# Seven-product up-projection of a hybrid decoder layer: weight tiles counted one by one, parts of x and gated pieces formed and loaded at other places

## Chip, core and metric

The kernel runs on one core of a Trainium2 chip. The metric is the device time of one execution in microseconds (us); lower is better. TensorE (PE in the profile) does the matrix products, VectorE (DVE) and ScalarE (ACT) the elementwise work, GpSimd (POOL) a little, and SyncE (SP) issues most DMAs. Each engine executes its own instructions in the order in which the program lists them, and waits for the others through semaphores.

## The reference, cut to what matters

One decoder layer runs on 1024 prompt tokens and 8 single-token samples (T = 1024, TT = 1032 columns in all). The change touches the layer's second half: the layer norm after the mixers, a gated feed-forward network with a causal convolution of width 3, and the entry of its down-projection.

```python
x = layer_norm(ALPHA * x + mix, ln1_g, ln1_b)
hup = x @ w_up                                  # D_MODEL 1024 -> 2 * D_FF, D_FF = 2816 = 22 * 128
c = ext[:, 0:L]*conv_w[0] + ext[:, 1:L+1]*conv_w[1] + ext[:, 2:L+2]*conv_w[2] + conv_b
a, b = jnp.split(c, 2, axis=-1)
f = (jax.nn.gelu(a) * b) @ w_down
x = layer_norm(ALPHA * x + f, ln2_g, ln2_b)
```

## The kernel before, in words

**Products.** Activations stand transposed, features on partitions and the 1032 tokens in columns. Every fp32 operand is split into a high and a low part (`hi` by a copy on ACT, `lo = x - hi` on DVE), and each product is three matmuls: hi with hi, hi with lo, lo with hi. The tile `xhi`/`xlo` holds eight feature tiles of 1032 columns.

**Order of work.** The program is written by hand. A list of units (`run_units`) and later the loops `run_pairs` and `run_down` issue the matmuls. Two side lanes hold Python generators. `side.advance(us)` is called after about each 0.6 us worth of matmuls and gives both lanes that much credit; a generator's `yield 4.0` means "go on 4 us of TensorE work later". Evacuations of PSUM and the steps of the convolution (`post`) are issued at the end of each chunk of columns. So a yield sets only the place of an instruction in its engine's queue. When it runs is set by the queue ahead of it and by its operands.

**The layer norm** (`to_features`, L380 to L396). Rows are transposed by TensorE, scaled by ACT into `tmp` (L389), stored to DRAM (`x1D`, a DMA issued by ACT, L392), copied to `xhi` by ACT (L393) and subtracted to `xlo` by DVE (L394), for eight feature tiles in each of three passes over token columns. The up-projection of the columns starts when the last pass is through.

**Plain up-projection.** The first three of 22 column tiles (each with an a and a b half) are computed plainly, as units of 24 matmuls in each of three chunks (384, 384 and 264 columns). Here they are called 0a, 0b, 1a, 1b, 2a, 2b. Their PSUM tiles have the tag "d" with 3 buffers, so a chunk needs the evacuation (`hup`, ACT, L1524) of the third chunk before it. Before unit 1a, `open_ffn` opens the pools of this stage and puts `g_parts` in lane 0 and `g_first` in lane 1. Pool "wf" has NWF = 12 tiles.

**Seven-product up-projection.** The other 19 column tiles use a Strassen-like scheme: x and w are cut into 2 by 2 blocks and seven products (numbers 1 to 7) replace eight. `g_parts` forms the parts of x for products 6, 7 and 4 (tiles `tx`): for each of four feature tiles k it loads four quarters from `x1D` and forms differences on DVE (L1672 to L1680) and splits them (L1664 ACT, L1665 DVE). `last_part` (L1688 to L1693) splits the difference that product 5 needs into the right half of `xhi`/`xlo`, which unit 2b still reads. For a pair of column tiles (a and b) four weight tiles are loaded, three more are sums (DVE adds at L1585, L1588, L1590 and one in place at L1593), and `prepare()` splits one of the seven per call (L1600 ACT, L1601 DVE) into one of seven slots. A pair runs in two halves of 258 columns, each with products in the order 1, 2, (3 of the half before), 6, (4 of the half before), 7, 5. Products 6, 5 and 3 add onto the PSUM bank of product 1, and product 4 onto that of product 7, after what stood there has been read. The block in the lower right (`c22`, DVE, L1759) is read from the bank of product 7 before product 4 goes onto it.

**Counting.** `made["live"]` counts "wf" tiles. A pair counts 6 (four loads and two sums) from its load to its last prepare; nothing of it is loaded until all 6 fit.

**Down-projection.** The gated rows (`gD` in DRAM) are loaded in groups of four (`stage`, L1850) and split into `xhi`/`xlo` (L1854 ACT, L1855 DVE). For the first group the eight pieces are loaded into "wf" tiles and placed during the last half of the last pair (`early_stage`; L1870, L1874, L1875); the tiles of `x1D` for the residual (`z2`, L1862) are loaded there too, four at a time. `run_down` adds each output chunk onto `z2` (L1934, L1936).

Of the kernel before, what the change touches and what calls it, by code (L numbers as in the profile page):

```python
# [8 lines left out]
F32 = mybir.dt.float32  # L9
# [103 lines left out]
def tile_hybrid_step(ctx: ExitStack, tc: tile.TileContext, x_prompt, mem_prompt, x_sample, cache_mem_k,  # L113
# [1436 lines left out]
    wq, made = [], {"load": 0, "key": 0, "obj": 0, "step": 0, "live": 0}  # L1550
# [3 lines left out]
    class Weights:  # L1554


        def __init__(self, src, steps=(0,)):
            self.src, self.w, self.f, self.steps = src, {}, {}, steps
            self.nf = 6 if len(src) > 1 else 1
# [4 lines left out]
    def load_weights():  # L1564
        while made["load"] < len(wq) and made["live"] + wq[made["load"]].nf <= NWF:
            o = wq[made["load"]]
            for key, src in o.src.items():
                o.f[key] = wf_tile(src.shape[1] * 128)
                nc.sync.dma_start(o.f[key].rearrange("p (k c) -> p k c", c=128), src)
            made["live"] += o.nf  # L1570
            made["load"] += 1

    def prepare():
# [5 lines left out]
        if made["obj"] == made["load"]:  # L1579
            return False  # L1580
        if len(o.src) > 1:
            f, add = o.f, nc.vector.tensor_add
            if key == 1:
                f[5] = wf_tile()
                add(f[5], f[21], f[4])  # L1585
            elif key == 2:
                f[6] = wf_tile()
                add(f[6], f[5], f[1])  # L1588
            elif key == 6:
                add(f[21], f[1], f[21])  # L1590
                f[7] = f.pop(21)
            elif key == 3:
                add(f[2], f[2], f[6])  # L1593
                f[3] = f[2]
# [7 lines left out]
        o.w[key] = [x.rearrange("p (k c) -> p k c", c=128) for x in (hi, lo)] + [slot]  # L1602
        made["step"] += 1
        if made["step"] == len(o.steps):
            made["live"] -= o.nf
            o.f.clear()
            made["step"] = 0
            made["obj"] += 1
# [19 lines left out]
    def open_ffn():  # L1628
# [10 lines left out]
        made["live"] = 8  # L1639
# [8 lines left out]
    def g_parts():  # L1648
# [5 lines left out]

        def load(k):
            quarters[k] = []
            for a in range(2):
                for b in range(2):
                    x = wf_tile(HT)
                    nc.sync.dma_start(x, x1D[k + 4 * a][:, b * HT:(b + 1) * HT])  # L1660
                    quarters[k].append(x)
# [5 lines left out]
        load(0)  # L1667
        yield 4.0
        load_weights()
        for k in range(4):  # L1670
# [4 lines left out]
            yield 1.5  # L1675
            split(7, k, x22)
            V.scalar_tensor_tensor(x11, x22, -1.0, x11, op0=OP.mult, op1=OP.subtract)
            yield 1.7
            split(6, k, x11)
            V.scalar_tensor_tensor(x21, x11, -1.0, x21, op0=OP.mult, op1=OP.subtract)  # L1680
            yield 1.7
            split(4, k, x21)
            if k < 3:
                load(k + 1)
                yield 4.0
        made["live"] -= 4

    def last_part():  # L1688
        for k in range(4):
            h, l = xhi[:, k, HT:], xlo[:, k, HT:]  # L1690
            nc.scalar.activation(h, N1[k], AF.Copy)
            nc.vector.tensor_sub(l, N1[k], raw_f(h))
        made["live"] -= 4  # L1693
# [110 lines left out]
    def run_pairs():  # L1804
        before = None
        halves_ = [Half(u, s) for u in pairs for s in range(2)]
        for i, h in enumerate(halves_ + [None]):
            if i == len(halves_) - 3:
                made["live"] += 8
            for x, (m, old) in enumerate(ORDER):  # L1810
                hh = before if old else h
                if hh is None:
                    continue
# [3 lines left out]
                if m == 4 and hh.s:  # L1817
                    post.append(conv_pair(hh.u.j, hh.u.out))
                if x in (2, 3, 5, 6):
                    post[:] = [g for g in post if next(g, g) is not g]  # L1820
# [3 lines left out]
                if i == len(halves_) - 1:  # L1824
                    early_stage(m)
# [18 lines left out]
    def stage_load(gi, parts):  # L1844
        j0, nk = GROUPS[gi]
        if gi not in stage:
            stage[gi] = place["t"].tile([128, 4, TT], F32, tag="t", name=nm("stage"))
        for c0, c1 in parts:
            for k in range(nk):
                nc.sync.dma_start(stage[gi][:, k, c0:c1], gD[j0 + k][:, c0:c1])  # L1850

# [5 lines left out]
    def load_z2(fs):  # L1857
        for f in fs:
            if f % 4 == 0:
                Z2["t", f // 4] = place["t"].tile([128, 4, TT], F32, tag="t", name=nm("z2"))  # L1860
            Z2[f] = Z2["t", f // 4][:, f % 4]
            nc.sync.dma_start(Z2[f], x1D[f])  # L1862

    piece = {}

    def early_stage(m):

        def fetch(k, b):
            x = piece[k, b] = wf_tile(HT)
            nc.sync.dma_start(x, gD[k][:, b * HT:(b + 1) * HT])  # L1870

        def place_piece(k, b):
            c = slice(b * HT, (b + 1) * HT)
            nc.scalar.activation(xhi[:, k, c], piece[k, b], AF.Copy)  # L1874
            nc.vector.tensor_sub(xlo[:, k, c], piece[k, b], raw_f(xhi[:, k, c]))  # L1875

        if m == 1:
            assert made["live"] - 4 <= NWF, made
            for k in range(4):
                fetch(k, 0)  # L1880
        elif m == 2:
            assert made["live"] <= NWF, made
            for k in range(4):
                fetch(k, 1)
        elif m == 6:
            place_piece(0, 0)
            load_z2(range(4))
        elif m == 4:
            place_piece(1, 0)
        elif m == 7:  # L1890
            place_piece(2, 0)
            load_z2(range(4, 8))
        elif m == 5:
            place_piece(3, 0)
            for k in range(4):
                place_piece(k, 1)
            made["live"] -= 8
# [54 lines left out]
    downs[0].before = lambda: side.add(0, "stages", g_stages())  # L1952
# [69 lines left out]
    last_part()  # L2022
# [40 lines left out]
```

## Time and profile before

| what | value |
|---|---|
| median of 3 runs | 2209.15 us (2208.63 to 2210.41) |
| profiled execution | 2208.31 us, span of its instructions 2206.6 us |
| TensorE busy | 2135.5 us, 97% of the span |
| mean granted clock of TensorE | 0.984 of full speed |
| DVE, ACT busy | 1286.8 us (58%), 857.4 us (39%) |

TensorE is busy in all but 71 us of the span. The granted clock is the share of its full speed (2.4 GHz) that TensorE was given, and has two levels, full and half; a mean between them says how much of a stretch was at half.

### The profile page before, as it was taken

Reading aid. Unit: us, or ns where it says so; the run is one execution under the profiler, and the core shown is the slowest. Engines: PE = TensorE matmul, PEld = TensorE weight load, DVE = VectorE, ACT = ScalarE, POOL = GpSimd, SP = SyncE. Lnnn points to the kernel's source line nnn. Section 1 sums busy time; section 2 is a strip of 40 time slices with the busy share of each in tenths; the row PEclk is TensorE's granted clock in tenths of the full one; section 3 lists DMA queues with packets and bytes.
Section 4 is the critical chain, followed back from the end, with each engine's and each line's share of the span. In section 5 each row is a group of like instructions: output and inputs, shape, how many; then the busy total and the mean of one; then the engine's idle time right before and its main releaser. Section 6 shows DMA issues by size and latency. Waiting matters only on the chain.

```text
span 2206.6 us, 37536 instructions
## 1 busy us (share of the span) xinstructions
PE 2135.5 (97%) x14801; PEld 2088.6 (95%) x14801; DVE 1286.8 (58%) x2898; ACT 857.4 (39%) x1717; POOL 207.9 (9%) x329
## 2 busy tenths in 40 slices
PE   7999999999999999999999999998999999999996
PEld 7999999999998999899999999887999999899995
DVE  5734738373756754534335555556777777755357
ACT  4624343434446433332213334543445445522111
POOL 5301010101000000000005610000000000000004
PEclk8999999999999999999999999988999999999998
DMA  8231232223378665649644233333232232651302
GB/s 240 79 107 53 58 72 53 63 59 72 90 184 270 199 203 173 196 142 377 199 136 130 60 96 96 115 116 97 59 88 82 64 88 69 205 168 65 111 1 77
DMA packets 303836, 265.53 MB, mean 120 GB/s; under 512 B 19405, under 2 KB 275753, under 8 KB 303645
## 3 DMA queue, kind: packets, MB, share of 16 engines
q1 hardware_dynamic: 286763, 244.06, 37.1%
q10 hardware_dynamic: 16898, 19.09, 2.5%
q8 instruction: 116, 1.90, 0.4%
q14 instruction: 59, 0.48, 0.1%
HBM read 197.21 MB, written 66.49 MB: 120 GB/s over the span
## 4 chain that ended last, share of the span: by engine, by line
PE 82%; DVE 6%; ACT 4%; DMA 3%; POOL 2%; issue 2%; SPq 1%; ACTq 0%; POOLq 0%; DVEq 0%
PE pd L258 47%; PE pd L1743 15%; PE pd L1926 10%; PE ps L675 1%; PE ps L676 1%; PE ps L677 1%; DMA g2r<-gD 1%; PE ps L699 1%; DVE wlo L189 1%; DVE whl L1601 1%; DMA Cs<-in_state_C_dram 1%; POOL ps L1283 1%; ACT whi L188 1%; DMA wf<-x1D 1%; PE ps L387 1%
## 5 line engine op out<-in xcount | busy, mean ns | idle before, releaser
L258 PE MATMUL pd<-xhi,whi 128*128 128x384 f32 (+1 forms) x1872 | 607.2, 324 | 5.2 <-ACT hup L1524 5.2
L258 PE MATMUL pd<-xlo,whi 128*128 128x384 f32 (+1 forms) x1872 | 604.3, 323 | 0.0
L258 PE MATMUL pd<-xhi,wlo 128*128 128x384 f32 (+1 forms) x1872 | 601.3, 321 | 0.0
L258 PEld LDWEIGHTS pd<-xhi,whi 128*128 128x128 f32 x1872 | 353.6, 189 | 14.8 <-issue 8.3
L258 PEld LDWEIGHTS pd<-xlo,whi 128*128 128x128 f32 x1872 | 353.5, 189 | 1.8 <-issue 1.7
L258 PEld LDWEIGHTS pd<-xhi,wlo 128*128 128x128 f32 x1872 | 353.3, 189 | 1.8 <-issue 1.7
L189 DVE TENSOR_TENSOR wlo<-raw,whi 128x512 fp32r<-128x512 f32 (+1 forms) x236 | 166.5, 737 | 278.0 <-ACT whi L188 272.1
L1926 PE MATMUL pd<-xhi,whl 128*128 128x384 f32 (+3 forms) x1056 | 251.3, 324 | 8.5 <-DVE z L1936 5.0
L1743 PE MATMUL pd<-xhi,whl 128*128 128x258 f32 x1216 | 231.8, 287 | 6.9 <-DVE whl L1601 3.9
L1743 PEld LDWEIGHTS pd<-xhi,whl 128*128 128x128 f32 x1216 | 192.8, 191 | 12.1 <-DVE whl L1601 9.4
L1926 PEld LDWEIGHTS pd<-xhi,whl 128*128 128x128 f32 x1056 | 186.0, 191 | 10.0 <-DVE z L1936 6.2
L188 ACT ACTIVATE whi<-raw 128x512 fp32r<-128x512 f32 (+1 forms) x264 | 151.3, 615 | 100.3 <-PE pd L258 76.0
L1743 PE MATMUL pd<-tx,whl 128*128 128x258 f32 x1368 | 175.0, 286 | 9.2 <-DVE hup L1759 4.7
L1743 PEld LDWEIGHTS pd<-tx,whl 128*128 128x128 f32 x1368 | 169.5, 191 | 10.3 <-DVE hup L1759 5.0
L1600 ACT ACTIVATE whl<-wf 128x512 fp32r<-128x512 f32 (+1 forms) x181 | 107.5, 617 | 183.3 <-PE pd L1926 152.0
L1743 PE MATMUL pd<-xlo,whl 128*128 128x258 f32 x608 | 172.9, 284 | 0.0
L1926 PE MATMUL pd<-xlo,whl 128*128 128x384 f32 (+3 forms) x528 | 170.6, 323 | 0.0
L371 POOL TENSOR_TENSOR rs<-rs,half 128x1 f32<-128x1 f32 (+2 forms) x60 | 36.9, 614 | 1243.2 <-DVE rs L370 1212.3
L1601 DVE TENSOR_TENSOR whl<-wf,whl 128x512 fp32r<-128x512 f32 (+1 forms) x181 | 121.7, 674 | 29.7 <-ACT whl L1600 29.3
L1743 PEld LDWEIGHTS pd<-xlo,whl 128*128 128x128 f32 x608 | 116.3, 191 | 0.0
L1936 DVE TENSOR_TENSOR z<-pd,z 128x384 f32<-128x384 f32 (+3 forms) x120 | 60.8, 513 | 87.8 <-PE pd L1926 87.8
L1781 DVE SCALAR_TENSOR_TENSOR cv<-hup,colB,cv 128x1023 f32<-128x1023 f32 x76 | 97.2, 1279 | 15.2 <-ACT cv L1772 15.2
(557 smaller groups left out, 3753.7 us busy)
## 6 DMA issues: line engine op xcount, KB each, us to landing
raw<-in_w_in_dram SPq DMA_DIRECT2D x72, 512.0 KB
wf<-in_w_up_dram SPq DMA_DIRECT2D x76, 256.0 KB
gD<-cv SPq DMA_DIRECT2D x22, 516.0 KB
wf<-in_w_down_dram SPq DMA_DIRECT2D x40, 256.0 KB
stage<-gD SPq DMA_DIRECT2D x18, 516.0 KB
raw<-in_w_o_dram SPq DMA_DIRECT2D x18, 512.0 KB
mx<-mixD SPq DMA_DIRECT2D x16, 516.0 KB
raw<-in_w_mem_kv_dram SPq DMA_DIRECT2D x16, 512.0 KB
```

What stands on the lines that cost most here:

```text
L188: nc.scalar.activation(s.hi[:, ks], s.raw[:, ks], AF.Copy)
L189: (nc.gpsimd if s.pool else nc.vector).tensor_sub(s.lo[:, ks], s.raw[:, ks], raw_f(s.hi[:, ks]))
L258: nc.tensor.matmul(p[:u.m, :n], lhsT=a, rhs=b, start=j == 0, stop=j == len(seq) - 1)
L371: nc.gpsimd.tensor_tensor(out=rs[:n], in0=rs[:n], in1=half[:n], op=OP.pow)
L387: nc.tensor.transpose(p[:, j * 128:j * 128 + m], t[:m, f * 128:(f + 1) * 128], ident[:m, :m])
L675: nc.tensor.matmul(out, lhsT=wh, rhs=xh, start=first, stop=False)
L1600: nc.scalar.activation(hi, src, AF.Copy)
L1601: nc.vector.tensor_sub(lo, src, raw_f(hi))
L1743: nc.tensor.matmul(p, lhsT=a[:, k], rhs=b, start=onto is None and k + n == 0, stop=k == 3 and n == 2, skip_group_check=onto is not None)
L1781: nc.vector.scalar_tensor_tensor(a, b, w, a, op0=OP.mult, op1=OP.add)
L1926: nc.tensor.matmul(p[:, :n], lhsT=a[:, k], rhs=b, start=k + i == 0, stop=k == nk - 1 and i == 2)
L1936: nc.vector.tensor_add(z, p[:, :n], z)
```

## The change

Six edits. In `to_features`, for the layer norm before the feed-forward network (not for the input norm), the copy to `xhi` goes from ACT to DVE. Weight tiles are counted and loaded one by one, up to 10 of 12 tiles, and each is given up when it has been split; the sums have a function of their own, which `g_first` can call ahead. `open_ffn` counts 6 tiles for x in place of 8. `g_parts` loads its quarters in halves, loads weights after the first four quarters, and waits 10 us of credit in place of 4 before the first difference; `g_first` starts at 12 in place of 4. `last_part` splits one feature tile at a time, between the products of the first half. At the end, the eight gated pieces are loaded as tiles come free over the last two halves, four are placed in the last half and four after it, `z2` is loaded one tile at a time, and the next stage is loaded one tile at a time from 10 us of credit on (its first split at 34 in place of 8).

```diff
@@ to_features
-            nc.scalar.activation(xhi[:, f, c0:c0 + n], tmp[:, :n], AF.Copy)
+            if b0 == LIB:
+                nc.scalar.activation(xhi[:, f, c0:c0 + n], tmp[:, :n], AF.Copy)
+            else:
+                nc.vector.tensor_copy(xhi[:, f, c0:c0 + n], tmp[:, :n])
@@ load_weights, sum_weights, prepare
-        while made["load"] < len(wq) and made["live"] + wq[made["load"]].nf <= NWF:
+        while made["load"] < len(wq) and made["live"] + made["hold"] < NWF - 2:
             o = wq[made["load"]]
-            for key, src in o.src.items():
-                o.f[key] = wf_tile(src.shape[1] * 128)
-                nc.sync.dma_start(o.f[key].rearrange("p (k c) -> p k c", c=128), src)
-            made["live"] += o.nf
-            made["load"] += 1
+            key = tuple(o.src)[made["key"]]
+            o.f[key] = wf_tile(o.src[key].shape[1] * 128)
+            nc.sync.dma_start(o.f[key].rearrange("p (k c) -> p k c", c=128), o.src[key])
+            made["live"] += 1
+            made["key"] += 1
+            if made["key"] == len(o.src):
+                made["key"] = 0
+                made["load"] += 1
+    def sum_weights(o, n):
+        f, add = o.f, nc.vector.tensor_add
+        while o.sums < n:
+            if made["obj"] == made["load"]:
+                return False
+            if o.sums == 0:
+                f[5] = wf_tile()
+                add(f[5], f[21], f[4])
+            elif o.sums == 1:
+                f[6] = wf_tile()
+                add(f[6], f[5], f[1])
+            else:
+                add(f[21], f[1], f[21])
+                f[7] = f.pop(21)
+            o.sums += 1
+        return True
...
+        made["live"] -= key in (6, 7, 3, 4, 0)
@@ open_ffn
-        made["live"] = 8
+        made["live"] = 6
@@ g_parts
         load(0)
+        yield 6.0
+        load_weights()
         yield 4.0
-        load_weights()
...
             split(7, k, x22)
+            if k < 3:
+                load_half(k + 1, 0)
...
             split(4, k, x21)
             if k < 3:
-                load(k + 1)
-                yield 4.0
-        made["live"] -= 4
+                load_half(k + 1, 1)
+                yield 3.5
+        made["live"] -= 2
+        load_weights()
@@ g_first
-        yield 4.0
+        yield 12.0
+        n = 0
         while not made.get("open"):
-            if not prepare():
+            o = wq[0]
+            if prepare():
+                yield 1.5
+            elif made["load"] and o.sums < 3 and sum_weights(o, o.sums + 1):
+                yield 1.5
+            else:
                 load_weights()
-            yield 3.0
+                yield 1.0
@@ run_pairs
-            if i == len(halves_) - 3:
-                made["live"] += 8
+            if i == len(halves_) - 2:
+                made["hold"] = 8
...
+                if i == 0 and last_part.k < 4:
+                    last_part()
...
-                if i == len(halves_) - 1:
-                    early_stage(m)
+                if i >= len(halves_) - 2:
+                    early_stage(i - len(halves_) + 2, m)
@@ early_stage
+        while todo and made["live"] < NWF - 2 * (i == 0):
+            k, b = todo.pop(0)
+            piece[k, b] = wf_tile(HT)
+            nc.sync.dma_start(piece[k, b], gD[k][:, b * HT:(b + 1) * HT])
+            made["live"] += 1
+            made["hold"] -= 1
...
+        if i == 1:
+            if m in (6, 4, 7, 5):
+                place_piece((6, 4, 7, 5).index(m), 0)
+            if m == 6:
+                load_z2(0)
+        elif i == 2:
+            for k in range(2):
+                place_piece(k + 2 * (m == 4), 1)
+            load_z2(1 + (m == 4))
+            load_weights()
+    def g_z2():
+        for f in range(3, 8):
+            load_z2(f)
+            yield 5.0
@@ g_stages
         ready.append("stage0")
+        yield 10.0
...
-            stage_load(gi, ((0, TT),))
-            yield 8.0
-            for k in range(GROUPS[gi][1]):
+            for k in range(nk):
+                nc.sync.dma_start(stage[gi][:, k], gD[j0 + k])
+                yield 5.0 if gi == 1 else 2.0
+            yield 4.0
+            for k in range(nk):
                 stage_split(gi, k, 0, TT)
                 yield 4.0
```

## Rows read from the trace of the kernel before

**Rows 1.** Busy time by stretch: length, engines with counts, PE clock, DMA share, GB/s.
```profile
1380.00:1418.00 38.00, 33.30 (x273) 32.56 (x271) 25.55 (x57) 20.38 (x36) 1.64 (x3) 1.00 0.42 125
...
1480.00:1491.00 11.00, 11.00 (x72) 11.00 (x72) 8.44 (x14) 5.55 (x11) 0.00 (x0) 1.00 0.10 25
...
1503.00:1527.00 24.00, 14.39 (x67) 12.86 (x68) 12.33 (x21) 8.14 (x16) 0.00 (x0) 0.64 0.44 129
...
1800.00:1860.00 60.00, 59.89 (x497) 59.32 (x497) 44.22 (x76) 31.00 (x62) 0.00 (x0) 1.00 0.28 81
...
1911.00:1919.00 8.00, 3.26 (x17) 3.05 (x16) 5.11 (x8) 4.98 (x10) 0.00 (x0) 0.75 1.00 357
1919.00:1934.00 15.00, 15.00 (x88) 14.87 (x88) 11.84 (x20) 5.22 (x8) 0.00 (x0) 0.91 1.10 338
1934.00:1943.00 9.00, 5.54 (x28) 5.25 (x27) 6.98 (x10) 3.97 (x5) 0.00 (x0) 0.81 1.09 329
```

**Rows 2.** TensorE in order of time: start, us, instruction, [idle before <- what ended it].
```profile
1461.05 0.33 PE L258 MATMUL pd<-xhi,whi 128*128 128x384 f32 x1
...
1470.61 0.69 PE L258 MATMUL pd<-xhi,whi 128*128 128x384 f32 x1 [5.20 <-ACT hup L1524]
...
1520.83 0.58 PE L1743 MATMUL pd<-tx,whl 128*128 128x258 f32 x1 [3.18 <-ACT whl L1600]
...
1916.17 0.58 PE L1743 MATMUL pd<-tx,whl 128*128 128x258 f32 x1 [4.74 <-DVE hup L1759]
...
1937.77 0.44 PE L1926 MATMUL pd<-xhi,whl 128*128 128x384 f32 x1 [3.46 <-DVE z L1934]
```

**Rows 3.** DVE's first difference of x, then ACT, in order of time.
```profile
1468.81 0.70 DVE L1672 TENSOR_TENSOR wf<-wf,wf 128x516 f32<-128x516 f32 x1 [8.31 <-DMA wf<-x1D]
...
1469.54 0.63 ACT L1664 ACTIVATE tx<-wf 128x516 fp32r<-128x516 f32 x1 [13.03 <-DVE wf L1672]
...
1526.40 0.39 ACT L1749 ACTIVATE v<-pd 128x258 f32<-128x258 f32 x1 [5.10 <-PE pd L1743]
```

**Rows 4.** SP's queue in order of time: start, us of issuing.
```profile
1460.33 19.03 SPq L1660 DMA_DIRECT2D wf<-x1D  x16
...
1499.51 2.05 SPq L1569 DMA_DIRECT2D wf<-in_w_up_dram  x4
```

**Rows 5.** Groups by line, 1461 to 1527: busy us, mean ns, idle before.
```profile
L1665 DVE TENSOR_TENSOR tx<-wf,tx 128x516 fp32r<-128x516 f32 x12 | 8.3, 695 | 5.5 <-ACT tx L1664 5.5
L1491 DVE SCALAR_TENSOR_TENSOR cv<-hup,colB,cv 128x1022 f32<-128x1022 f32 x4 | 5.1, 1278 | 0.0
...
L1601 DVE TENSOR_TENSOR whl<-wf,whl 128x512 fp32r<-128x512 f32 x5 | 3.4, 685 | 4.7 <-ACT whl L1600 4.7
...
L1692 DVE TENSOR_TENSOR xlo<-wf,xhi 128x516 fp32r<-128x516 f32 x4 | 2.5, 689 | 0.0
L1491 DVE SCALAR_TENSOR_TENSOR cv<-stT,colB,cv 128x8 f32<-128x8 f32 x8 | 1.8, 224 | 0.1
...
L1485 ACT ACTIVATE cv<-hup,colB 128x1032 f32<-128x1032 f32 x4 | 5.0, 1238 | 0.0
```

**Rows 6.** DVE and ACT at the end of the pairs, in order of time.
```profile
1911.52 1.22 DVE L1795 TENSOR_TENSOR cv<-cv,cv 128x1032 f32<-128x1032 f32 x1
1912.66 3.11 DVE L1875 TENSOR_TENSOR xlo<-wf,xhi 128x516 fp32r<-128x516 f32 x5
1915.70 0.42 DVE L1759 SCALAR_TENSOR_TENSOR hup<-pd,v 128x258 f32<-128x258 f32 x1
...
1934.93 1.06 ACT L1854 ACTIVATE xhi<-stage 128x1032 fp32r<-128x1032 f32 x1 [3.75 <-DMA stage<-gD]
...
1936.02 1.23 DVE L1855 TENSOR_TENSOR xlo<-stage,xhi 128x1032 fp32r<-128x1032 f32 x1 [2.93 <-ACT xhi L1854]
```

**Rows 7.** A subtraction of the layer norm's last pass, and a DVE copy's group.
```profile
1439.67 0.43 DVE L394 TENSOR_TENSOR xlo<-tmp,xhi 128x256 fp32r<-128x256 f32 x1 [0.74 <-ACT xhi L393]
...
L956 DVE CAST k<-xq 128x128 fp32r<-128x128 f32 x64 | 14.0, 219 | 0.0
```

More of the change, by code (lines that the diff above doesn't have):

```diff
@@ L1542, in tile_hybrid_step @@
     units[n0 + 2:n0 + 2] = tail
-    wq, made = [], {"load": 0, "key": 0, "obj": 0, "step": 0, "live": 0}
+    wq, made = [], {"load": 0, "key": 0, "obj": 0, "step": 0, "live": 0, "hold": 0}
     slots = []
@@ L1558, in __init__ @@
             self.src, self.w, self.f, self.steps = src, {}, {}, steps
-            self.nf = 6 if len(src) > 1 else 1
+            self.sums = 0
     def wf_tile(n=512):
@@ L1578, in prepare @@
         key = o.steps[made["step"]]
-        if made["obj"] == made["load"]:
-            return False
[L1581 to L1594, printed above, removed]
+        if len(o.src) > 1:
+            if not sum_weights(o, {1: 1, 2: 2}.get(key, 3)):
+                return False
+            if key == 3:
+                nc.vector.tensor_add(o.f[2], o.f[2], o.f[6])
+                o.f[3] = o.f[2]
+        elif key not in o.f:
+            return False
         slot = slots.pop(0)
@@ L1653, in g_parts, with load_half @@
         quarters = {}
-        def load(k):
[L1656 to L1661, printed above, removed]
+        def load_half(k, a):
+            for b in range(2):
+                x = wf_tile(HT)
+                nc.sync.dma_start(x, x1D[k + 4 * a][:, b * HT:(b + 1) * HT])
+                quarters.setdefault(k, []).append(x)
+        def load(k):
+            load_half(k, 0)
+            load_half(k, 1)
         def split(m, k, src):
@@ L1812, in run_pairs @@
                 if hh is None:
+                    if last_part.k < 4:
+                        last_part()
                     continue
@@ L1818, in run_pairs @@
                     post.append(conv_pair(hh.u.j, hh.u.out))
+                if i == 0 and last_part.k < 4:
+                    last_part()
+                    if x == 3:
+                        load_weights()
                 if x in (2, 3, 5, 6):
@@ L1842, in down_weights @@
         return w
[L1844 to L1850, printed above, removed]
     def stage_split(gi, k, c0, c1):
@@ L1855, in stage_split, with early_stage @@
         nc.vector.tensor_sub(xlo[:, kk, c0:c1], stage[gi][:, k, c0:c1], raw_f(xhi[:, kk, c0:c1]))
[L1857 to L1862, printed above, removed]
-    piece = {}
[L1866 to L1870, printed above, removed]
+    piece = {}
+    todo = [(k, b) for b in range(2) for k in range(4)]
+    def early_stage(i, m):
+        while todo and made["live"] < NWF - 2 * (i == 0):
[4 more added lines that the diff above has]
+            made["hold"] -= 1
         def place_piece(k, b):
@@ L1874, in place_piece, with load_z2 @@
             nc.scalar.activation(xhi[:, k, c], piece[k, b], AF.Copy)
[L1875 to L1897, printed above, removed]
+            nc.vector.tensor_sub(xlo[:, k, c], piece.pop((k, b)), raw_f(xhi[:, k, c]))
+            made["live"] -= 1
+        if i == 1:
[7 more added lines that the diff above has]
+            load_z2(1 + (m == 4))
+            load_weights()
+    def load_z2(f):
+        if f % 4 == 0:
+            Z2["t", f // 4] = place["t"].tile([128, 4, TT], F32, tag="t", name=nm("z2"))
+        Z2[f] = Z2["t", f // 4][:, f % 4]
+        nc.sync.dma_start(Z2[f], x1D[f])
+    def g_z2():
+        for f in range(3, 8):
+            load_z2(f)
+            yield 5.0
     def g_stages():
         ready.append("stage0")
+        yield 10.0
         for gi in range(1, len(GROUPS)):
@@ L1903, in g_stages @@
                 yield 1.0
-            stage_load(gi, ((0, TT),))
-            yield 8.0
-            for k in range(GROUPS[gi][1]):
+            j0, nk = GROUPS[gi]
+            stage[gi] = place["t"].tile([128, 4, TT], F32, tag="t", name=nm("stage"))
+            for k in range(nk):
[3 more added lines that the diff above has]
+            for k in range(nk):
                 stage_split(gi, k, 0, TT)
@@ L1950, in tile_hybrid_step @@
         downs += [Down(gi, f, down_weights(gi, f)) for f in range(8)]
-    downs[0].before = lambda: side.add(0, "stages", g_stages())
+    downs[0].before = lambda: (side.add(0, "stages", g_stages()), side.add(1, "z2", g_z2()))
     gb = {}
```

23 lines of the change are left out of this document (12 added, 11 removed).

## Prediction

> **What bounds the kernel now.** Read the table first: TensorE is busy in 97% of the span, so a change pays only where TensorE stands still or runs at half clock. Then the busy time by stretch [rows 1]. In the middle of the pairs (1800 to 1860) TensorE is busy 59.89 of 60 us at full clock: nothing is to be won there. From 1503 to 1527 it is busy 14.39 of 24 us, at a mean clock of 0.64. From 1911 to 1919 it is busy 3.26 of 8 us, and from 1934 to 1943 5.54 of 9 us, at 0.75 and 0.81.
>
> Next TensorE in order of time, where the brackets name what ended each stall [rows 2]: 5.20 us at 1470.6 for an evacuation by ACT, 3.18 us at 1520.8 for a weight copy (the last of several waits at the start of the pairs), 4.74 us at 1916.2 for DVE's read of c22, 3.46 us at 1937.8 for DVE's addition to z.
>
> Then why each was late. DVE's first difference of x waits until 1468.81 for the quarters of x, which SP issued from 1460.33 on [rows 3, 4]. ACT stood 13.03 us before the copy behind that difference [rows 3]; the evacuation is queued behind that copy, hence the 5.20 us. The first pair's weights are issued at 1499.51 only [rows 4], because six tiles must fit and the parts of x hold eight; so nearly all splitting of these weights falls between 1503 and 1527. At the end, five subtractions of gated pieces, 3.11 us, and a product of 1.22 us stand before c22 on DVE [rows 6]. The 3.46 us come from a stage split whose load had not landed: ACT waited 3.75 us for the DMA, and DVE's subtraction of 1.23 us stood before the addition [rows 6].
>
> **Layer norm copies.** 24 copies go from ACT to DVE. The trace has no DVE copy of 256 or 384 columns; 128 columns take 0.219 us, and the subtraction of 256 columns 0.43 [rows 7]. I take 0.3, nearer to the copy. In the last pass DVE waits 0.74 us for ACT's copy per feature tile [rows 7]; with its own copy it has the result 0.44 us earlier, 8 x 0.44 = 3.5 us at most. The same pass has transposes on TensorE that take their turn, and the copies cost DVE 24 x 0.3 = 7 us in all. Bounds: a gain of 3.5, and a loss of 2.4 (8 x 0.3) where DVE ends the wait. I take a gain of 1.0.
>
> The row that speaks against this edit: from 1380 to 1418 DVE is the busier one, 25.55 of 38 us against ACT's 20.38 [rows 1]. The Trainium skill ("Perfetto Trace Analysis", Optimizing Scalar/DVE Operations) says that work may be given to ScalarE where DVE is saturated, which is the opposite of this edit. By that rule this term would be the loss of 2.4 and the sum below 3.4 us smaller.
>
> **From unit 1b to the fifth product of the first pair.** In the kernel before this takes from 1461.05 [rows 2] to 1526.40, when ACT evacuates product 5 [rows 3]. What TensorE needs is three units of 11 us (72 matmuls in 11.00 us at full clock [rows 1]) and five products of 1.45 (12 matmuls each; 497 in 60 us [rows 1]): 40.3 us, so 1501.4. The quarters still arrive at 1468.8: SP's order before them is the same. After that everything hangs on DVE, whose list up to product 5 is:
> - 28 differences and low parts of x at 0.695: 19.5 [rows 5]
> - 2 low parts for unit 2b's weights and 11 sums and low parts for the first pair, at 0.685: 8.9 [rows 5]
> - the convolutions of 1a, 1b and 2a, each 2 x 1.28 + 2 x 0.22 = 3.0: 9.0 [rows 5]; one product of 1.22 [rows 6]
> - `last_part`, 4 x 0.69 = 2.8 [rows 5], and one evacuation of 0.42 [rows 6].
>
> That is 41.8 us for 59 instructions. Back to back they overlap (four of 0.689 took 2.5 us, about 0.08 less each [rows 5]): 41.8 - 58 x 0.08 = 37.2. DVE's waits for ACT's copies of the parts were 5.5 us [rows 5]. The weights' work, now placed between, may fill them, but I leave them in: 1468.8 + 37.2 + 5.5 = 1511.5, and 0.6 for the last three matmuls of product 5: 1512.1, a gain of 14.3. With all waits filled it would be 1506.6.
>
> TensorE is not much earlier. The first differences now stand about 10.6 us of credit into this stage, so ACT's blocked copy comes behind the evacuations of 1a, and the stall of 5.20 goes from that place. But what is late next is the evacuation of 1b's first chunk: behind DVE's six instructions to the second difference (1468.8 + 6 x 0.62 = 1472.6) ACT has a copy of x (0.63), a weight copy (0.62) and the convolution's start (1.24 [rows 5]) before it, so it ends near 1475.5. Unit 2a wants that bank at 1461.05 + 11.1 = 1472.2: a stall of 3.3 us, and up to 2.8 us lost to half clock, as after c22's stall now (below). 1501.4 + 3.3 + 2.8 = 1507.5. So DVE decides, and the gain is at most 18.9. The lower bound: `g_first` puts the first sums, which need the second and third weight tile, before the second part of x. These tiles are issued right behind the quarters, four in 2.05 us [rows 4], and should land with 1472; if they don't, DVE and ACT stand still with all that is queued, evacuations too. I bound that by the 6 us which the quarters take now beyond their issue (1468.8 less 1460.3 and 2.1): gain 8.
>
> **End of the pairs and start of the down-projection.** With four of the five subtractions moved behind c22, it comes 4 x 0.62 = 2.5 us earlier: the stall goes from 4.74 to 2.3, a gain of 2.4. After the stall the clock was at half: 2.83 us of matmuls up to 1919 give back 1.4, and 0.09 x 15 us after 1919 give 1.35 [rows 1]. I count both, since the 4.7 idle us between 1380 and 1418 left the clock at 1.00 [rows 1]. The stage's loads now have over 20 us before their split, so the 3.46 us go, and 0.19 x 9 = 1.7 us of half clock after them [rows 1]. Sum 10.3. What replaces them: the last split of the second stage (46 us of credit against 45.4 for the first group) and that of the last stage (25 against 22.7) fall behind the boundary of their group. Each is bounded by 1.06 + 1.23 us [rows 6] below nothing; three of four feature tiles go ahead meanwhile, so I take 0.5 each. Gain 9.3; if the c22 stall stays as long as now, 5.
>
> **At nothing.** Loading `z2` and the pieces one by one costs the same bytes, under TensorE's work: DVE needs `z2[1]` 5.7 us after `z2[0]`. Sums and splits of the other 18 pairs are the same instructions in the same places.
>
> **Sum.** 1.0 + 14.3 + 9.3 = 24.6. Against the profiled execution's own 2208.3 (the median is 2209.15): 2183.7, said as 2184 us.
>
> **The rivals.**
> 1. *DVE becomes the bound and evacuations suffer.* For it: the list above leaves DVE no pause for 40 us, ACT's evacuations stand behind copies that wait for it, and the layer norm loads it more. It would be the loss of 2.4, a gain of 8, and 5 at the end: 10.6, so 2197.7. Against it: before, DVE was idle for 11.7 of the 24 us up to 1527 [rows 1].
> 2. *The pairs pay.* Slower: a tile that is loaded alone arrives after its prepare, the slot is missed, and a split stands before a product in each of 19 pairs. One such wait cost 3.18 us [rows 2]: 60 us, so 2244. It decides from (24.6 + 4.4) / 19 = 1.5 us per pair on. For it: TensorE has no slack there. Against it: ten tiles are two and a half pairs, some 50 us of work ahead (168 matmuls a pair, 497 in 60 us).
> 3. *It does not do what it says.* The last part of x, not the weights, paces the start of the pairs, and the new stall at 2a eats the old one; only 5 at the end remain, and the layer norm loses 2.4: 2205.7.
>
> **Chances.** Forecast 0.60 (2177 to 2192), rival 1 0.27 (2192 to 2202), rival 3 0.06, rival 2 0.07. A measurement of this kernel tells 0.2% (4.4 us) from no change. Faster: forecast, rival 1 and part of rival 3, 0.88; same 0.05; slower 0.07. The upper bounds of the three gains together (3.5 + 18.9 + 10.3 = 32.7) would give 2175.6, which I don't expect all at once; the other end reaches into rival 1: 2177 to 2200.
>
> **What would show it.** In the changed profile: the first weight loads of a pair issued within 5 us of the first quarters; DVE nearly without idle time from 1468 to 1510; product 5 of the first half evacuated by 1512; no stall of 5 us in unit 1b, but one of about 3 us before 2a; c22's stall about 2.3 us and full clock after it; none at the second stage. Stalls repeating every 20 us in the pairs, a wait of DVE for weight DMAs of several us near 1472, or a clock that falls after the c22 stall all the same would make the prediction wrong.

## The result, and the profile after

The changed kernel took 2179.38 us (median of 4 runs, 2178.32 to 2181.64), the kernel before 2209.78 us beside it: ratio 0.9864, 95% interval 0.9847 to 0.9881. On a second chip the same pair gave 0.9869 (0.9850 to 0.9888). Forecast were 2184 us and a gain of 24.6; the gain of the medians is 30.4. The first profiled execution of the changed kernel took 2181.64 us, the longest of its four, and its span is 2179.9; against the profiled kernel before it gains 26.7.

First the busy time by stretch of that execution, with the columns of [rows 1]. The second row runs from the first matmul of the pairs to ACT's copy of product 5 of the first half.

```profile
1380.00:1418.00 38.00, 34.37 (x279) 33.66 (x278) 28.26 (x64) 17.48 (x29) 1.64 (x3) 1.00 0.42 126
1498.96:1511.94 12.98, 9.05 (x64) 8.24 (x63) 12.25 (x20) 8.83 (x17) 0.00 (x0) 0.91 0.61 185
1800.00:1860.00 60.00, 60.00 (x502) 59.92 (x501) 46.46 (x77) 30.66 (x60) 0.00 (x0) 1.00 0.25 81
1890.00:1900.00 10.00, 7.15 (x42) 6.73 (x42) 8.17 (x15) 6.94 (x14) 0.00 (x0) 0.83 0.69 219
1900.00:1920.00 20.00, 20.00 (x128) 19.85 (x127) 15.55 (x27) 5.42 (x8) 0.00 (x0) 1.00 1.09 340
```

The same stretch of the kernel before:

```profile
1503.30:1526.40 23.10, 13.79 (x62) 12.26 (x63) 12.15 (x20) 7.45 (x15) 0.00 (x0) 0.63 0.45 131
```

So the start of the pairs has shrunk from 23.1 us, 9.3 of them with TensorE standing still, to 13.0 us with 3.9. The stall at the second stage has gone: from 1900 to 1920 TensorE is busy throughout. In the middle of the pairs 502 matmuls stand in 60 us where [rows 1] had 497, though TensorE counted as busy then too. The weight loads (PEld) of the two rows tell them apart: 59.32 us busy before, 59.92 now.

Next TensorE's remaining stalls in order of time, in answer to [rows 2].

```profile
1474.25 0.44 PE L258 MATMUL pd<-xhi,whi 128*128 128x384 f32 x1 [3.34 <-ACT hup L1527]
...
1503.13 3.13 PE L1776 MATMUL pd<-tx,whl 128*128 128x258 f32 x24 [1.11 <-ACT t L1782]
...
1508.65 0.39 PE L1776 MATMUL pd<-xlo,whl 128*128 128x258 f32 x1 [1.52 <-DVE xlo L1716]
...
1510.46 0.58 PE L1776 MATMUL pd<-xlo,whl 128*128 128x258 f32 x1 [1.18 <-DVE xlo L1716]
...
1895.62 2.95 PE L1776 MATMUL pd<-tx,whl 128*128 128x258 f32 x12 [2.32 <-DVE hup L1792]
```

The 5.20 us of unit 1b are gone, and 3.34 us stand before unit 2a. Product 6 waits 1.11 us until ACT has read product 1 from the bank that it adds onto (`t`), and product 5 waits for `last_part` (L1716). The c22 stall has halved. SP's queue and ACT's copy of product 5 answer to [rows 3, 4]:

```profile
1458.72 2.38 SPq L1676 DMA_DIRECT2D wf<-x1D  x4
1461.15 2.89 SPq L1573 DMA_DIRECT2D wf<-in_w_up_dram  x4
```

```profile
1511.94 0.39 ACT L1782 ACTIVATE v<-pd 128x258 f32<-128x258 f32 x1 [3.28 <-PE pd L1776]
```

**How the runs are compared.** At 1390 of the kernel before, ahead of all that the change moves but some of the layer-norm copies, the runs lie between 2.2 us early and 5.4 us late, so medians tell a few us apart only roughly. The table therefore gives what each profiled execution gains on the profiled kernel before within four stretches. They end at the same instructions: S0 from a statistic of the layer norm (1390.3 before) to the evacuation of the first chunk of unit 1a (1456.05), the last ahead of unit 1b in the kernel before; S1 from there to v, ACT's copy of product 5, of the third half (1546.84); S2 to the last v (1909.28); S3 to the first plain addition of the down-projection (1973.73). "Clock" is the mean granted clock of S1, and of S3 with the last 22 us ahead of it; before it was 0.87 and 0.94. The forecast of S1 reaches to product 5 of the first half only.

| run | median us | ratio to before (95%) | S0 | S1 | S2 | S3 | S1 to S3 | clock |
|---|---|---|---|---|---|---|---|---|
| forecast | 2184 | | 1.0 | 14.3 | 0 | 9.3 | 23.6 | |
| changed | 2179.38 | 0.9864 (0.9847, 0.9881) | 2.5 | 11.0 | 5.5 | 8.6 | 25.1 | 0.94, 0.98 |
| after_again | 2178.83 | 0.9869 (0.9850, 0.9888) | 1.1 | 13.6 | 5.5 | 10.0 | 29.1 | 0.98, 1.00 |
| e1_behind | 2184.15 | 0.9870 (0.9853, 0.9886) | 1.1 | 15.6 | 0.0 | 10.0 | 25.6 | 0.98, 1.00 |
| e2_weights_late | 2190.35 | 0.9901 (0.9886, 0.9916) | -0.3 | 9.6 | 0.0 | 8.5 | 18.0 | 0.94, 0.98 |
| e3_parts_early | 2187.71 | 0.9888 (0.9873, 0.9902) | 2.5 | 6.4 | 5.5 | 10.0 | 21.8 | 0.94, 1.00 |
| e4_stage_early | 2184.29 | 0.9872 (0.9857, 0.9886) | 1.1 | 12.1 | 5.5 | 5.2 | 22.8 | 0.93, 0.98 |
| e5_pieces_before_c22 | 2185.92 | 0.9885 (0.9870, 0.9901) | 2.6 | 11.5 | 5.5 | 6.0 | 23.0 | 0.96, 0.98 |
| e6_copy_act | 2181.16 | 0.9875 (0.9858, 0.9892) | 0.4 | 11.0 | 5.5 | 8.6 | 25.1 | 0.94, 0.98 |
| e7_c22_first | 2178.19 | 0.9867 (0.9847, 0.9887) | -0.3 | 13.6 | 5.5 | 11.4 | 30.4 | 0.98, 1.00 |
| e8_next_pair_later | 2179.72 | 0.9857 (0.9840, 0.9873) | 1.1 | 16.0 | 5.5 | 10.0 | 31.4 | 0.98, 1.00 |
| e9_behind_then_ahead | 2177.01 | 0.9861 (0.9839, 0.9882) | 2.0 | 16.3 | 5.2 | 8.5 | 29.9 | 0.98, 0.98 |
| e10_both | 2177.49 | 0.9848 (0.9833, 0.9863) | 2.6 | 16.1 | 5.2 | 11.6 | 32.8 | 0.98, 1.00 |
| e11_both_first_late | 2180.55 | 0.9866 (0.9846, 0.9887) | 2.6 | 11.0 | 5.2 | 11.5 | 27.7 | 0.94, 1.00 |

The two executions of the changed kernel differ by 3.9 us in S1 to S3 and agree in S2. So stretches are compared below at like clocks. Even then they scatter: e4 and e6 leave the instructions of S1 as changed and gain 12.1 and 11.0 there at clocks of 0.93 and 0.94, and e1, e9 and e10, which have the same instructions in S1, gain 15.6 to 16.3 at 0.98. A difference in S1 of less than about 1 us shows nothing by itself.

### The profile page after: what moved, and what is told of

Its sections match the earlier page's. It is cut to its first block, busy times and chain, and to the rows that moved or that the text cites. A ratio compares the mean times of both kernels' runs of the same rounds, so it can differ in the third digit from the quotient of the medians.

```text
span 2179.9 us, 37597 instructions
## 1 busy us (share of the span) xinstructions
PE 2123.8 (97%) x14801; PEld 2081.2 (95%) x14801; DVE 1296.2 (59%) x2922; ACT 847.2 (39%) x1693; POOL 207.7 (10%) x329
## 4 chain that ended last, share of the span: by engine, by line
PE 85%; DVE 6%; DMA 2%; POOL 2%; ACT 2%; issue 2%; SPq 1%; ACTq 0%; POOLq 0%; DVEq 0%
PE pd L258 48%; PE pd L1776 17%; PE pd L1960 10%; PE ps L678 1%; PE ps L679 1%; PE ps L680 1%; DVE wlo L189 1%; DMA ck<-in_cache_mem_k_dram 1%; PE ps L702 1%; DMA Cs<-in_state_C_dram 1%; POOL ps L1286 1%; DMA wf<-x1D 1%; PE ps L387 0%; ACT whi L188 0%; PE ps L883 0%
## 5 line engine op out<-in xcount | busy, mean ns | idle before, releaser
L1618 DVE TENSOR_TENSOR whl<-wf,whl 128x512 fp32r<-128x512 f32 (+1 forms) x181 | 122.0, 675 | 46.5 <-ACT whl L1617 46.1
```

The source lines that it names most:

```text
L1618: nc.vector.tensor_sub(lo, src, raw_f(hi))
```

## Experiments

Theory A explains S2 by the place of the weight splits among the products, S1 by VectorE's list, S3 by two queues. The chain of waits of the kernel before, in the middle of the pairs (start, us, what), shows where S2 could come from:

```profile
1567.68 0.40 ACT v L1749
...
1568.11 0.43 DVE hup L1759
1568.53 0.61 DVE wf L1593
1569.14 0.38 ACT t L1749
1569.52 0.53 ACT whl L1600
...
1570.07 0.70 DVE whl L1601
...
1570.82 17.29 PE pd L1743 x142
```

Once per pair product 3 waits for its weight, which is summed (L1593) behind c22 (L1759), which waits for v. TensorE's matmul record hides it, since matmul ends are modelled. The chain of the changed kernel there is TensorE alone:

```profile
1564.96 24.37 PE pd L1776 x203
1589.33 0.44 PE ps L1512 x4
```

**e1_behind**

```diff
-                if x in (0, 1, 4) or x == 3 and h and h.s:
+                if (x in (0, 1, 4) or x == 3 and h and h.s) and not (i < 2 and x < 2):
```

> Four calls of the splitting of weights are left out at the start of the pairs, so that every pair's splits fall half a pair later, where they fell in the kernel before; the loads, the parts of x and the stages stay as changed. Theory A (the splits of a pair, and of key 3 above all, run four ahead now and no longer stand in the chain v, c22, sum of key 3, t, split, product 3): the changed kernel's gain of 0.30 us a pair is lost, so +5.4 us against it, about 2185 us; some 497 matmuls in 60 us of the pairs in place of 502, and the chain of waits goes through VectorE and ScalarE once a pair again. Rival B (the gain per pair comes from weight tiles counted and loaded singly): no change, within 1 us.

S2 gains 0.0 in place of 5.5, and the busy time by stretch shows the matmuls of before:

```profile
1800.00:1860.00 60.00, 59.83 (x495) 59.13 (x494) 44.78 (x76) 30.29 (x60) 0.00 (x0) 1.00 0.23 71
```

Its chain has the pieces c22, sum, t, split, product 3 again, of which these are two:

```profile
1574.06 0.61 DVE wf L1608
...
1575.59 0.70 DVE whl L1618
```

Tile by tile loading was left in, so rival B falls. Not expected: S1 gained 2.0 us more than the second run of the changed kernel at the same clock, so being ahead costs something at the start (e9, below, has the same start). VectorE's group of splits up to product 5 shows what: nine of them in the changed kernel, seven here.

```profile
L1618 DVE TENSOR_TENSOR whl<-wf,whl 128x512 fp32r<-128x512 f32 x9 | 6.1, 684 | 0.7 <-ACT whl L1617 0.7
```

```profile
L1618 DVE TENSOR_TENSOR whl<-wf,whl 128x512 fp32r<-128x512 f32 x7 | 4.7, 689 | 0.7 <-ACT whl L1617 0.7
```

**e2_weights_late**

```diff
-        made["live"] = 6        # open_ffn
+        made["live"] = 10
-        made["live"] -= 2       # end of g_parts
+        made["live"] -= 6
```

> The count of live tiles begins at 10, so that no weight is loaded or summed until the parts of x are done; all else as changed. Theory A (VectorE's list of work between the opening of the up-projection and the last part sets when product 5 of the first pair can run, and weights worked on early only fill that list): sums and splits of the first pair's weights come after the parts, product 5 some 7 to 12 us later, and the splits of the pairs half a pair behind again, up to +5.4 us; +7 to +17 us in all. Rival B (the loads of x's parts pace product 5 and the weights are worked on in their shadow either way): within 2 us.

The first pair's weights are issued behind the parts of x again, as in [rows 4], though only 37.1 us after the evacuation that opens S1, where the kernel before took 43.5:

```profile
1496.44 3.54 SPq L1573 DMA_DIRECT2D wf<-in_w_up_dram  x6
```

S1 is 1.5 to 2.6 us below the executions with S1 as changed at a like clock (11.0 to 12.1), far less than the 7 to 12 expected of product 5, and S2 is 0.0: the splits are half a pair behind. Together that is 7 to 8 us, so the sum reaches the low end of theory A only by the loss in S2, and most of what theory A expected of the start did not come. Working on weights early is worth little at the start; most of what it buys is the place in the pairs. It also means that weights issued behind the parts don't by themselves explain the slow start of the kernel before: with them S1 still gains 9.6.

**e3_parts_early**

```diff
-        yield 6.0
+        yield 2.0
         load_weights()
-        yield 4.0
+        yield 2.0
```

> The first difference of x's quarters is formed 6 us of TensorE work earlier, about where the kernel before formed it; weights loaded as changed. Theory A (VectorE's list decides): a stall of some 5 us comes back in unit 1b, behind copies that wait for the quarters, and as much of the time is won where product 5 waits; product 5 of the first pair ends within 2 us of the changed kernel's, and the time is +0 to +3 us. Rival B (the late start of the parts is itself the gain): +5 to +7 us.

The stall in 1b comes back, larger than in [rows 2]:

```profile
1473.85 0.69 PE L258 MATMUL pd<-xhi,whi 128*128 128x384 f32 x1 [7.91 <-ACT hup L1527]
```

S1 gains 6.4, 4.7 less than the first run of the changed kernel at 0.94. Theory A as written (0 to 3) fails, rival B (5 to 7) is nearer. Two of VectorE's rows show where time goes:

```profile
1494.55 0.70 DVE L1685 TENSOR_TENSOR tx<-wf,tx 128x516 fp32r<-128x516 f32 x1 [1.79 <-ACT tx L1684]
...
1498.18 0.70 DVE L1693 TENSOR_TENSOR wf<-wf,wf 128x516 f32<-128x516 f32 x1 [1.74 <-DMA wf<-x1D]
```

The list is the same, but its waits are not. Between the first difference and 1500 VectorE stands 5.6 us, against 2.9 in the second run of the changed kernel (0.70, 1.22, 0.30 and 0.70). That the parts now come before there is weight work to put between is the likely reason; no run tests it by itself.

**e4_stage_early**

```diff
         ready.append("stage0")
-        yield 10.0
@@ for k in range(nk):
             nc.sync.dma_start(stage[gi][:, k], gD[j0 + k])
-            yield 5.0 if gi == 1 else 2.0
-        yield 4.0
+        yield 8.0
```

> The loads of the second group of gated pieces stand as in the kernel before, all at once as soon as the down-projection opens, and their splits 8 us of TensorE work after; all else as changed. Theory A (the splits on ScalarE and VectorE wait for loads that are late, and the first evacuations of the down-projection are queued behind them): a stall of 3.5 us at the first change of accumulator comes back, with 1.7 us at half clock: +4 to +6 us. Rival B (the stall goes because the up-projection ends at another time): within 1 us.

The stall is back at 3.30 us ([rows 2] had 3.46):

```profile
1914.58 0.69 PE L1958 MATMUL pd<-xhi,whl 128*128 128x384 f32 x1 [3.30 <-DVE z L1966]
```

S3 gains 5.2: 3.5 less than the changed kernel at the same 0.98, 4.8 less than at 1.00. Theory A holds.

**e5_pieces_before_c22**

```diff
+            if m == 5:                          # last half
+                for k in range(4):
+                    place_piece(k, 1)
-            for k in range(2):                  # behind it
-                place_piece(k + 2 * (m == 4), 1)
```

> The four splits of the second halves of the first gated pieces stand ahead of the last c22 again, as in the kernel before, in place of two behind each of the last two products; all else as changed. Theory A (VectorE's order decides when c22 frees the accumulator that product 4 of the last half needs): the stall there grows from 2.3 to 4.7 us, +2.4 us against the changed kernel, up to +4 with a longer stretch at half clock. Rival B (the splits wait for their loads there, or the stall has another cause): within 1 us.

```profile
1901.32 0.90 PE L1776 MATMUL pd<-tx,whl 128*128 128x258 f32 x4 [4.75 <-DVE hup L1792]
```

4.75 us, where [rows 2] had 4.74; S3 gains 2.6 less than the changed kernel at the same clock. Theory A holds: VectorE's order it is.

**after_again, e6_copy_act, e7_c22_first, e9_behind_then_ahead** ran on one chip, after_again being the changed kernel itself.

> The changed kernel as it is, on the chip of the runs sent with it. All theories: 0.985 to 0.988 of the time before, and in its trace the same stretches as the first time: 11.0 us gained between the last evacuation of the unit before the parts (1456) and the third half of the pairs, 5.4 us over the pairs, 7 to 10 us from the last product 5 to the first plain additions of the down-projection, the spread being one stretch at half clock (1.4 to 1.7 us).

S2 and S3 came as expected, S1 not: 13.6 in place of 11.0. The stalls are nearly the same, 3.16 us before 2a and 2.32 at c22, but the clock is not.

```profile
1472.35 0.44 PE L258 MATMUL pd<-xhi,whi 128*128 128x384 f32 x1 [3.16 <-ACT hup L1527]
...
1891.35 0.87 PE L1776 MATMUL pd<-tx,whl 128*128 128x258 f32 x5 [2.32 <-DVE hup L1792]
```

The busy time by stretch, around the stall before 2a and around that of c22, in the first run and then in the second:

```profile
1470.00:1490.00 20.00, 16.66 (x96) 16.46 (x95) 17.99 (x29) 10.35 (x19) 0.00 (x0) 0.91 0.36 107
...
1890.00:1900.00 10.00, 7.15 (x42) 6.73 (x42) 8.17 (x15) 6.94 (x14) 0.00 (x0) 0.83 0.69 219
```

```profile
1470.00:1490.00 20.00, 17.35 (x106) 16.99 (x107) 17.97 (x28) 11.19 (x22) 0.00 (x0) 1.00 0.37 109
...
1890.00:1900.00 10.00, 8.65 (x57) 8.65 (x58) 8.98 (x17) 6.85 (x12) 0.00 (x0) 1.00 0.95 271
```

**e6_copy_act**

```diff
-            if b0 == LIB:
-                nc.scalar.activation(xhi[:, f, c0:c0 + n], tmp[:, :n], AF.Copy)
-            else:
-                nc.vector.tensor_copy(xhi[:, f, c0:c0 + n], tmp[:, :n])
+            nc.scalar.activation(xhi[:, f, c0:c0 + n], tmp[:, :n], AF.Copy)
```

> The copies of the second layer norm's parts go back to ScalarE; all else as changed. Theory A (the two tail units' evacuations on ScalarE were queued behind these copies and are no more): the 2.4 us that the changed kernel wins between the last layer-norm evacuation (1433.3 in the trace of before) and the first tail evacuation (1445.7) are lost, so +1 to +2.4 us. Rival B (a copy is dearer on VectorE, whose work is then late): no change, or up to 2.4 us faster than the changed kernel.

S0 gains 0.4 here and 1.1 in each of the four runs with the copies on VectorE and the same clock of 0.95 (after_again, e1, e4, e8; the kernel before has 0.95 too): a difference of 0.7 us. The trace has a place for it. TensorE waits for an addition to z that stands on VectorE behind a subtraction, and that one waits for ACT's copy:

```profile
1416.10 0.56 DVE L394 TENSOR_TENSOR xlo<-tmp,xhi 128x384 fp32r<-128x384 f32 x1 [0.71 <-ACT xhi L393]
...
1417.51 0.33 PE L1395 MATMUL ps<-ident,z 128*128 128x128 f32 x1 [0.93 <-DVE z L1382]
```

In after_again TensorE waits 0.28 us there. But e9 waits 0.91 there with the copies on VectorE, so one execution without the copies doesn't settle a difference of this size. The 2.4 of the expectation is wrong: it was read between rows that don't answer to each other. From the evacuation at 1429.1 to the next but one (1445.7) these kernels run the same matmuls without a pause (the trace has 107 or 108 of them), and the clock tells them apart. Busy time by stretch of the kernel before, of e6_copy_act, and of e5_pieces_before_c22:

```profile
1429.10:1445.70 16.60, 16.60 (x108) 15.49 (x107) 4.48 (x14) 7.29 (x16) 0.00 (x0) 0.79 0.31 96
```

```profile
1428.60:1443.80 15.20, 15.20 (x107) 14.27 (x106) 4.51 (x14) 7.20 (x16) 0.00 (x0) 0.89 0.33 105
```

```profile
1434.10:1447.80 13.70, 13.70 (x108) 12.77 (x107) 6.31 (x20) 4.74 (x10) 0.00 (x0) 1.00 0.36 116
```

**e7_c22_first**

```diff
-                if before and (x == 0 or h is None and m == 3):
+                if before and x == 0:
                     before.c22()
+                if i == len(halves_) - 1 and m == 5:
+                    hh.c22()
```

> The last half's c22 is formed right behind its product 5 instead of one product later; all else as changed. Theory A (product 4 of the last half waits 2.3 us for the accumulator that c22 frees, and c22 is late only because VectorE has the splits of the gated pieces ahead of it): that stall goes, -2.3 us against the changed kernel, and -3.7 us where a stretch at half clock followed it. Rival B (the last products wait for the splits of the pieces or for the loads behind them anyway): within 1 us, the stall being named by another wait.

```profile
1893.05 1.70 PE L1776 MATMUL pd<-tx,whl 128*128 128x258 f32 x12 [0.57 <-DVE hup L1792]
```

The stall falls from 2.32 to 0.57 us, and S3 gains 1.4 more than after_again at the same clock: theory A, by less than its 2.3. The rest remains because c22 still stands on VectorE behind a step of the convolution and one subtraction of a piece, though v was done at 1890.72:

```profile
1890.63 1.28 DVE L1814 SCALAR_TENSOR_TENSOR cv<-hup,colB,cv 128x1022 f32<-128x1022 f32 x1
...
1891.96 0.69 DVE L1905 TENSOR_TENSOR xlo<-wf,xhi 128x516 fp32r<-128x516 f32 x1
1892.57 0.42 DVE L1792 SCALAR_TENSOR_TENSOR hup<-pd,v 128x258 f32<-128x258 f32 x1
```

In the medians the gain does not show.

**e9_behind_then_ahead**

```diff
-                if x in (0, 1, 4) or x == 3 and h and h.s:
+                if (x in (0, 1, 4) and not (i < 2 and x < 2) or x == 3 and h and h.s
+                        or x == 5 and 4 <= i < 8):
```

> The four calls of splitting left out at the start, as in the run above that stayed behind, and one call more in each of the halves 5 to 8, so that the splits are four ahead again from the third pair on. Theory A (early splits cost 4.6 us where VectorE's list sets product 5 of the first pair, and being ahead later is worth 0.30 us a pair): both are had, -15.6 us at the start and some -4.8 over the pairs, together about -4 us against the changed kernel. Rival B (the early gain of that run was the half clock that it happened not to have): the start wins what the changed kernel's wins, within 1.5 us, and the time is the changed kernel's within 1.5 us.

S1 gains 16.3, 2.7 more than after_again at the same clock, and S2 5.2: both are had. The 4.6 us which the expectation names had 2.6 us of difference between two runs of the changed kernel in it; the early splits cost 2.0 (e1) to 2.7 us (here). In the medians 1.8 us are left against after_again, between theory A's 4 and rival B's 1.5; in the profiled execution S3 has a stretch at half clock that after_again has not (8.5 for 10.0).

**e8_next_pair_later, e10_both, e11_both_first_late** ran with e5_pieces_before_c22 on one chip.

```diff
-                if x in (0, 1, 4) or x == 3 and h and h.s:
+                if x in ((5, 6) if i == 0 else (0, 1, 4)) or x == 3 and h and h.s:
```

> In the first half of the pairs the two splits for the next pair stand behind products 7 and 5 instead of behind products 1 and 2; as many splits, so that the later pairs stay four ahead. Theory A (these two splits stand ahead of the last parts of x on VectorE, and product 5 waits for those): the stalls of 0.4 to 1.5 and of 1.2 us within product 5 go, -1.5 to -2.7 us up to the third half, and the pairs win 5.4 us as in the changed kernel. Rival B (the last parts wait for the loads of x, or the stall moves to the splits that now come later): within 1 us.

No stall within product 5 is left; the one wait in the pairs' start is the one before product 6, for ACT's reading of product 1:

```profile
1508.87 3.48 PE L1776 MATMUL pd<-tx,whl 128*128 128x258 f32 x16 [2.20 <-ACT t L1782]
```

S1 gains 2.4 more than after_again, S2 the same 5.5. Theory A holds.

> The run that fell behind and then caught up, with c22 of the last half formed right behind its product 5. Theory A (the two gains lie in different stretches and add): -16.3 us up to the third half, -5.1 over the pairs, -11.3 to the down-projection, -32.7 in all from the evacuation at 1456, some 4 us under the second run of the changed kernel, about 2174 to 2175 us. Rival B (a gain in one stretch is eaten in the next): the time of the one edit alone, 2177 to 2178 us.

e10_both joins the edits of e9 and e7. 16.1, 5.2 and 11.6 make 32.8 before rounding (32.7 expected): the gains add. The median did not follow: 2177.49 us lies in rival B's range, on a chip where the kernel before took 2211.52 (2207.61 beside e7 and e9). The ratio, 0.9848, is the lowest of all; its interval overlaps those of the changed kernel, so the medians alone don't settle the 0.2% between them.

```diff
         yield 6.0
         load_weights()
-        yield 4.0               # g_parts
+        yield 7.0
-        yield 12.0              # g_first
+        yield 16.0
```

> As the run before it, with the first difference of x 3 us of TensorE work later and the first splits of weights 4 us later. Theory A (the stall of 2.7 to 3.3 us before unit 2a is one of the queue: the evacuation of 1b stands behind copies of the parts on ScalarE): that stall goes, and as VectorE's list is nearly full its work comes later by 1 to 3 us at products 6 to 5, so 0 to -2 us against the run before. Rival B (VectorE's list decides it all): what is won before 2a is lost at the products, 0 to +3 us.

For e11_both_first_late (the last diff above): the stall before 2a is gone, but a larger one stands at the start of the pairs, before product 6:

```profile
1508.95 1.44 PE L1776 MATMUL pd<-tx,whl 128*128 128x258 f32 x5 [8.21 <-ACT t L1782]
```

S1 loses 5.1 against e10_both, part of it clock (0.94 for 0.98). That is rival B's direction and more than its 3. Both ways off, earlier (e3) and later, cost more than the stall of about 3 us before 2a that they were about.

## Why the prediction was right, and what it missed

- **Layer norm copies, 1.0 forecast:** 0.7 measured, a size that the wait in e9 leaves unsettled. The 1.0 was picked between bounds of 3.5 and -2.4, so that it came near is in part luck. The subtraction no longer waits for ACT; VectorE's copy waits for ACT's scaling instead, as the groups by line of the changed kernel, 1380 to 1434, show (busy us, mean ns, idle before):

```profile
L397 DVE TENSOR_TENSOR xlo<-tmp,xhi 128x384 fp32r<-128x384 f32 (+1 forms) x12 | 6.2, 514 | 0.4
...
L396 DVE CAST xhi<-tmp 128x384 fp32r<-128x384 f32 (+1 forms) x12 | 4.0, 333 | 8.7 <-ACT tmp L389 8.7
```

  A copy takes 0.33 us (0.3 forecast). VectorE, busy 28.26 of 38 us now, still has room. The Trainium skill ("Perfetto Trace Analysis", Optimizing Scalar/DVE Operations) says that giving some work to ScalarE may make sense where DVE is saturated. With 25.55 of 38 us busy before and 28.26 now DVE was not, so the rule spoke neither for nor against this edit, and the loss of 2.4 did not come.
- **From 1b to product 5, 14.3 forecast:** from 1456.05 to the copy of product 5 the kernel before took 70.35 us, the changed one 57.50 (1454.44 to 1511.94), a gain of 12.9, and 13.4 in the second run. By the third half 11.0 and 13.6 were left, most of the difference being the clock. The mechanism was right: VectorE's list decides, and it has few pauses. Two sizes in it were off. The pauses for ACT's copies were 5.5 in the sum and are 1.4 behind the first difference (0.7 each at L1685 and L1618), plus 1.5 for DMAs; and two splits and two sums of the second pair, 4 x 0.69 = 2.8 us, stand in the list, which the sum did not count. The two errors, 2.6 and 2.8 us, cancel, so that the copy came at 1511.94 for 1512.1 forecast is in part luck. e9 and e8 moved the four away and won 2.7 and 2.4. How S1's gain divides among the edits is only partly shown: the late first difference is worth 4.7 us or more (e3), early weights 1.5 to 2.6 (e2), and no run took back the place of `last_part` or the halves of the quarters. So the reason that the prediction gave for the slow start, weights that were issued at 1499.51 only, explains the smaller part of the gain as far as the runs show.
- **The stall before 2a, 3.3 forecast:** 3.34 and 3.16, with the cause named.
- **End of pairs and start of down, 9.3 forecast:** 8.6 and 10.0. c22's stall was forecast at 2.3 and is 2.32; e5 put back its 2.4, and e4 a stall of 3.30 for the 3.46. The two terms of 0.5 for late splits did not come: TensorE lost 8.64 us standing still in S3 before and 2.76 after, which is the two stalls' 5.9, and from the end of S3 on both profiled executions took 232.9 us. Full clock after c22 came in the second run, not in the first: there the clock fell behind c22, one of the prediction's own signs of being wrong.
- **"Nothing is to be won there"** (the middle of the pairs): this step failed, by 5.5 us. It took 59.89 busy of 60 us for a limit, when the chain of waits had a path through v, c22, the sum and split of key 3 (product 3's weight) and product 3 in each pair. The row itself had a sign of it, weight loads busy 59.32 of 60 us, 59.92 when the wait is gone. The prediction also took the splits of the other 18 pairs to be "in the same places". They are not: with weights loaded and split among the parts of x, the calls of `prepare()` enter the pairs four ahead, and as a pair has seven calls and seven splits, they stay ahead. S2 is 17.5 pairs, so 5.5 us are 0.31 a pair. e1 and e2 took it away, e9 and e10 took it away at first and got it back.
- **Rival 2 (the pairs pay):** the pairs were indeed where the sum was incomplete, with the other sign; no weight came late. **Rival 1** did not come: VectorE became the bound of the start, as in the forecast, without a loss behind it. **Rival 3** would have left S1 as it was.

With the missed 5.5, the smaller start and the clock, 24.6 became 27.6 in the first pair of profiles (2.5 + 11.0 + 5.5 + 8.6), and 30.2 in the second (1.1 + 13.6 + 5.5 + 10.0). In the first pair the missed 5.5 and the 3.3 that S1 fell short offset each other in part: that the total came so near is luck to that extent. Why TensorE's clock falls behind a stall in one execution and not in another stays open.

## What to carry to other kernels

Count matmuls per us in a steady stretch and read its chain of waits before calling it full: a busy share of 99.8% hid 0.31 us in every pair, and the busy time of the weight loads gave a hint of it. A producer that runs ahead keeps its place in a loop whose calls match its work, so filling the queue once pays in every round; but work for the next round doesn't belong in the list that paces the first. Before trusting a difference of 1 to 4 us, run the same kernel twice and compare stretch by stretch at the same granted clock.

## What the runs showed of the hardware

- After stalls of the same length TensorE's clock may fall or not: around the 3.34 and 3.16 us before 2a the granted clock was 0.91 in one execution of the changed kernel and 1.00 in another, around the 2.32 us of c22 0.83 and 1.00. These two executions differ by 3.9 us in S1 to S3. Of nine executions with c22's stall at 2.32 or 2.33 us the clock fell right behind it in four (changed, e2, e6, e9) and stayed at 1.00 in five (after_again, e1, e3, e4, e8).
- The same matmuls (107 or 108 in the trace) took 16.60, 15.20 and 13.70 us at mean clocks of 0.79, 0.89 and 1.00.
